# Who makes the low half of a weight slab while the expert gates are built: VectorE alone, or VectorE and GpSimd in turn

## The chip, the cores and the metric

The program runs on one core of a Trainium2 chip. The time is device microseconds (us) of one execution; a run's time is the median of several executions, and 2389.93 us is the median of three runs of the kernel before. TensorE does the matrix products, VectorE (DVE in the profile) the elementwise work, ScalarE (ACT) the copies, roundings and activations, GpSimd (POOL) a second stream of elementwise work, and SyncE (SP) issues the transfers of weights.

## The reference, cut to what matters

Two blocks of a network run one after the other on 256 tokens of width 1024. The change is in the last part of the first block, the expert layer, which picks 16 of 16384 single-neuron experts per token and head:

```python
u = expert_u[ec]                                     # the chosen experts' input rows
a = jax.nn.gelu(jnp.einsum('cd,chkd->chk', xc, u), approximate=False) * wc
return jnp.einsum('chk,chkd->cd', a, expert_v[ec])   # wc: softmax over the 16 chosen
```

## The kernel before, in words

The kernel doesn't gather the chosen experts. It computes all 16384 as 128 slabs of 128 experts and multiplies the activations by a dense gate that is zero where an expert wasn't chosen. Per slab there are 24 matmuls on the input side (`u_pair`, two slabs each, lines 600 to 606) and 24 on the output side (`v_pair`, lines 739 to 766).

**A weight slab** is 128 by 1024 numbers in float32. Every product is made from two parts that TensorE takes: a rounded high half and the rest, the low half. `slab` (lines 93 to 101) loads a slab (SyncE, tile `raw`, five buffers), rounds it on ScalarE (tile `whi`, two buffers, line 99) and subtracts on VectorE, or on the engine given as `lo_eng` (tile `wlo`, two buffers, line 100):

```python
nc.scalar.activation(hi[:, :n], raw[:, :n], AF.Copy)
(lo_eng or nc.vector).tensor_tensor(lo[:, :n], raw[:, :n], hi[:, :n], op=ALU.subtract)
```

Of a slab's 24 matmuls the first 16 read the high half and the last 8 the low half.

**The gate** is built twice, `gate(0)` and `gate(1)`, each for 64 of the 128 slabs. A gate goes through the tokens in 16 blocks of 16. For a block VectorE makes two tiles of ones and zeros in float16 (`e1` from `i1T`, `e2` from `i2T`, line 718) and multiplies the second by the gate values (`ep`, line 722), all from inputs in SBUF. TensorE multiplies them in 32 small matmuls (line 731), 16 into bank B and 16 into bank E, and after each 16 VectorE multiplies the result into the activations (two instructions of line 737, one input in PSUM, one in SBUF). Banks B and E have one buffer each; `e1`, `e2` and `ep` have two.

**The weave.** `weave` takes a step of the gate (four small matmuls) and a step of the weights in turn. `gate(0)` is woven with 16 input pairs (six matmuls a step), so that a block of tokens and a pair of slabs go together. `gate(1)` is woven with 16 output pairs (four matmuls a step); about eleven of them go with the gate and the other five stand behind its end. A `v_pair` also splits its activations (ScalarE line 129, VectorE line 130, tile `wl`). Between the two gates, and behind the second, pairs run without a gate. The build of the program fixes one order of instructions for each engine, which may differ from the order of the code; on the chip each engine takes its instructions strictly in that order, and waits where an input isn't ready or a buffer isn't free.

GpSimd makes low halves before the gates (lines 688 and 694 and the query weights) and nothing from then until the second block.

Of the kernel before, what the change touches and what calls it, by code (L numbers as in the profile page):

```python
# [37 lines left out]
def chained(*gens):  # L38
    for g in gens:
        yield from g  # L40


def weave(*gens):

    live = list(gens)
    while live:
        live = [g for g in live if next(g, live) is not live]


class Builder:  # L50
# [525 lines left out]
    def peer(self, x, ss):  # L576
        nc, tc, a = self.nc, self.tc, self.a
# [5 lines left out]
        with tc.tile_pool(name="peer", bufs=1) as pool:  # L583
# [11 lines left out]
            def expert(n):  # L595

                o = 2 * n % QT
                return A[2 * n // QT][:, o:o + 2]

            def u_pair(n, lo_eng=None):  # L600
                bk = self.bank("g")
                for e in range(2):
                    s = self.slab(a["peer_u"][2 * n + e], lo_eng=lo_eng)
                    for u_pair.mm in self.mm3_steps(bk[:, e * T:(e + 1) * T], s, hh, hl):
                        yield
                u_pair.act = nc.scalar.activation(expert(n), bk[:, :].rearrange("p (e t) -> p e t", e=2), AF.Gelu)

            def u_run(lo, hi, lo_eng=None):
                for _ in chained(*(u_pair(n, lo_eng) for n in range(lo, hi))):
                    pass  # L610

            quarter(0)
# [1 line left out]
            with tc.tile_pool(name="topk", bufs=1) as tp:  # L614
# [11 lines left out]
                for j in range(8):  # L626
                    q = tp.tile([128, 2, T], F32, tag="q", bufs=2, name=self.nm("q"))
# [79 lines left out]
            with tc.tile_pool(name="gate", bufs=1) as gpool:  # L707
# [28 lines left out]
                                g = bk[:, :].rearrange("p (t i) -> p i t", t=8)[:, QT * q:QT * q + QT]  # L736
                                nc.vector.scalar_tensor_tensor(w, g, 1.0 / 32768.0, w, op0=ALU.mult, op1=ALU.mult)

                def v_pair(n):
                    wh = gpool.tile([128, 2, T], F32R, tag="wh", bufs=2, name=self.nm("wh"))  # L740
                    wl = gpool.tile([128, 2, T], F32R, tag="wl", bufs=2, name=self.nm("wl"))
                    self.split(wh, wl, expert(n))
                    end = n == NI // 2 - 1

                    def terms(e):
                        hi, lo = self.slab(a["peer_v"][:, 2 * n + e])
                        return [(vs, ws, e) for vs, ws in ((hi, wh), (hi, wl), (lo, wh))]

                    def add(db, p, vs, ws, e):
                        nc.tensor.matmul(acc[db // 2][:, (db % 2) * T:(db % 2 + 1) * T],  # L750
                                         vs[:, db * 128:(db + 1) * 128], ws[:, e],
                                         start=n == 0 and p == 0 and db % 2 == 0,
                                         stop=end and p == 5 and db % 2 == 1)

                    if end:
                        last = terms(0) + terms(1)
                        for db in range(NC):
                            for p in range(6):
                                add(db, p, *last[p])
                    else:  # L760
                        for e in range(2):
                            for p, t in enumerate(terms(e)):
                                for db in range(NC):
                                    add(db, 3 * e + p, *t)
                                    if db % 4 == 3:
                                        yield

                quarter(2, gpool, 1)
                q = QT // 2
                weave(gate(0), chained(*(u_pair(n) for n in range(2 * q, 3 * q))))  # L770
                acc = [self.bank("s") for _ in range(4)]
                for _ in chained(*(v_pair(n) for n in range(q))):
                    pass
                quarter(3)
                u_run(3 * q, 4 * q)
                weave(gate(1), chained(*(v_pair(n) for n in range(q, 2 * q))))
                for _ in chained(*(v_pair(n) for n in range(2 * q, 4 * q))):
                    pass
                x2 = x
# [770 lines left out]
```

## Time and profile before

| | us |
|---|---|
| median of three runs (2389.66 to 2403.57) | 2389.93 |
| the profiled execution | 2403.91 |
| its span, first to last instruction | 2401.9 |
| TensorE busy in the span | 2286.2 (95%) |
| VectorE busy | 1558.1 (65%) |
| GpSimd busy | 319.1 (13%) |
| `gate(0)`, first to last small matmul | about 528 to 647 |
| `gate(1)` | about 831 to 924 |
| output pairs behind it | 924 to 1136 |

All stretches are us from the span's start, in the one profiled execution. An instruction's time in a timeline row is from its start to its end; consecutive VectorE instructions overlap by a tenth of a us or less, so the cost of one in a full queue is the distance to the start of the next. "Idle before" in a row is what the engine waited, with what ended the wait.

### The profile page before, as it was taken

The numbers are of one execution on the slowest core, as the hardware profiler recorded it, in microseconds if no ns is written. First come the engines' busy times: TensorE is split into PE (matmuls) and PEld (weight loads), VectorE is DVE, ScalarE is ACT, GpSimd is POOL, SyncE is SP. The second block draws the span as 40 slices with busy tenths as digits, with TensorE's granted clock in tenths as the row PEclk, the third lists the DMA queues.
The fourth block names the chain that finished last, engine by engine and source line by source line (L and its number), as shares of the span: only waits on it lengthen the run. The fifth ranks groups of instructions, "written<-read, shape, count | busy, mean of one in ns | idle before, by whom it ended". The sixth has DMA issues, their size and how long they took to land.

```text
span 2401.9 us, 48629 instructions
## 1 busy us (share of the span) xinstructions
PE 2286.2 (95%) x20688; PEld 2171.1 (90%) x20688; DVE 1558.1 (65%) x2387; ACT 1086.7 (45%) x1501; POOL 319.1 (13%) x226
## 2 busy tenths in 40 slices
PE   4999898999999989999999789999999999999999
PEld 3888898999999989999999678878999999888999
DVE  7667579448854497555765777325665765787664
ACT  4344444443344433445544554423544644555543
POOL 3001379500000000000000543211000000101000
PEclk7889899999999999999999788967999999999999
DMA  7766444554455535555556222202556556433555
GB/s 252 243 197 201 150 159 158 189 180 141 143 187 187 179 115 163 187 185 167 175 185 178 83 91 64 84 1 70 181 181 187 182 185 184 155 106 107 185 185 148
DMA packets 107756, 378.33 MB, mean 158 GB/s; under 512 B 12113, under 2 KB 15697, under 8 KB 107410
## 3 DMA queue, kind: packets, MB, share of 16 engines
q1 hardware_dynamic: 104224, 370.52, 48.2%
q10 hardware_dynamic: 3314, 4.70, 0.6%
q8 instruction: 162, 2.65, 0.5%
q14 instruction: 56, 0.46, 0.1%
HBM read 374.12 MB, written 1.05 MB: 156 GB/s over the span
## 4 chain that ended last, share of the span: by engine, by line
PE 77%; DVE 6%; POOL 2%; ACT 1%; issue 1%; POOLq 0%; DVEq 0%; ACTq 0%
PE bkA L126 25%; PE bkA L572 15%; PE bkB L126 11%; PE bkC L750 10%; PE bkD L750 4%; DVE wlo L100 1%; POOL wlo L100 1%; POOL b L865 1%; PE bkC L1349 1%; DVE e L718 1%; PE bkA L1185 1%; ACT whi L99 1%; PE bkB L731 0%; PE bkE L731 0%; DVE ep L722 0%
## 5 line engine op out<-in xcount | busy, mean ns | idle before, releaser
L99 ACT ACTIVATE whi<-raw 128x1024 fp32r<-128x1024 f32 (+1 forms) x664 | 695.6, 1048 | 999.7 <-PE bkA L126 284.8
L100 DVE TENSOR_TENSOR wlo<-raw,whi 128x1024 fp32r<-128x1024 f32 (+1 forms) x606 | 733.4, 1211 | 480.1 <-ACT whi L99 449.7
L126 PE MATMUL bkA<-xh,whi 128*128 128x256 f32 x1336 | 332.0, 287 | 14.8 <-ACT whi L112 7.0
L126 PE MATMUL bkA<-xl,whi 128*128 128x256 f32 x1336 | 331.4, 288 | 12.4 <-POOL xl L316 6.3
L126 PEld LDWEIGHTS bkA<-xh,whi 128*128 128x128 f32 x1336 | 255.7, 192 | 18.2 <-ACT whi L112 7.7
L126 PEld LDWEIGHTS bkA<-xl,whi 128*128 128x128 f32 x1336 | 255.5, 193 | 16.3 <-POOL xl L316 8.7
L572 PE MATMUL bkA<-xh,whi 128*128 128x256 f32 x1024 | 259.9, 290 | 0.0
L572 PE MATMUL bkA<-xl,whi 128*128 128x256 f32 x1024 | 251.6, 281 | 0.0
L572 PEld LDWEIGHTS bkA<-xl,whi 128*128 128x128 f32 x1024 | 193.3, 189 | 0.0
L572 PEld LDWEIGHTS bkA<-xh,whi 128*128 128x128 f32 x1024 | 193.2, 189 | 0.0
L126 PE MATMUL bkA<-xh,wlo 128*128 128x256 f32 x1336 | 187.4, 282 | 2.5 <-DVE wlo L100 2.5
L100 POOL TENSOR_TENSOR wlo<-raw,whi 128x1024 fp32r<-128x1024 f32 x58 | 155.6, 2694 | 197.0 <-DVE on L149 128.7
L126 PEld LDWEIGHTS bkA<-xh,wlo 128*128 128x128 f32 x1336 | 171.0, 190 | 3.1 <-DVE wlo L100 2.9
L126 PE MATMUL bkB<-xh,whi 128*128 128x256 f32 x624 | 157.3, 289 | 1.9 <-ACT whi L99 1.1
L572 PE MATMUL bkA<-xh,wlo 128*128 128x256 f32 x1024 | 149.7, 284 | 7.5 <-POOL wlo L100 7.5
L126 PE MATMUL bkB<-xl,whi 128*128 128x256 f32 x624 | 156.2, 288 | 0.0
L572 PEld LDWEIGHTS bkA<-xh,wlo 128*128 128x128 f32 x1024 | 132.2, 188 | 8.9 <-POOL wlo L100 8.9
L190 POOL TENSOR_TENSOR sq<-sq,sq 128x256 f32<-128x256 f32 (+1 forms) x15 | 17.5, 1164 | 902.0 <-ACT sq L188 685.0
L126 PEld LDWEIGHTS bkB<-xh,whi 128*128 128x128 f32 x624 | 120.8, 194 | 2.6 <-ACT whi L99 1.4
L126 PEld LDWEIGHTS bkB<-xl,whi 128*128 128x128 f32 x624 | 120.8, 194 | 0.2 <-issue 0.2
L126 PE MATMUL bkA<-hh,whi 128*128 128x256 f32 x484 | 117.8, 282 | 0.0
L126 PE MATMUL bkA<-hl,whi 128*128 128x256 f32 x484 | 117.5, 281 | 0.0
(649 smaller groups left out, 4533.8 us busy)
## 6 DMA issues: line engine op xcount, KB each, us to landing
raw<-in_ffn_in_dram SPq DMA_DIRECT2D x176, 512.0 KB, 3.5
raw<-in_peer_u_dram SPq DMA_DIRECT2D x128, 512.0 KB, 3.3
raw<-in_peer_v_dram SPq DMA_DIRECT2D x128, 512.0 KB, 3.7
raw<-in_ffn_out_dram SPq DMA_DIRECT2D x64, 512.0 KB, 3.6
rawm<-in_w_mod_dram SPq DMA_DIRECT2D x48, 512.0 KB, 4.3
raw<-in_w_in_dram SPq DMA_DIRECT2D x36, 512.0 KB, 4.5
raw<-in_ffn_out_dram SPq DMA_DIRECT2D x32, 384.0 KB, 3.1
raw<-in_w_query_dram SPq DMA_DIRECT2D x16, 512.0 KB, 3.3
```

The source lines that it names most:

```text
L99: nc.scalar.activation(hi[:, :n], raw[:, :n], AF.Copy)
L100: (lo_eng or nc.vector).tensor_tensor(lo[:, :n], raw[:, :n], hi[:, :n], op=ALU.subtract)
L126: nc.tensor.matmul(out, w[:, i], x[k0 + i], start=first and n == 0, stop=last and n == 3 * kn - 1)
L190: (nc.vector if c % 2 else nc.gpsimd).tensor_tensor(acc[c % 2], acc[c % 2], t, op=ALU.add)
L572: last = nc.tensor.matmul(out, w[:, i], x[i], start=j == 0, stop=j == 3 * NC - 1)
L718: nc.vector.tensor_tensor(e, idx[:, ts].rearrange("p (a b) -> p a b", b=2)[:, :, None].to_broadcast(shape), iota[:, None, i0:i0 + e.shape[ ...
L750: nc.tensor.matmul(acc[db // 2][:, (db % 2) * T:(db % 2 + 1) * T], vs[:, db * 128:(db + 1) * 128], ws[:, e], start=n == 0 and p == 0 and d ...
L865: nc.gpsimd.tensor_tensor(ll[:, c], t, hh[:, c], op=ALU.subtract)
L1185: nc.tensor.matmul(by[er, i], UV[ch][:, h], PM[A][1][:, ch, 2 * i + e], start=True, stop=S is None)
L1349: nc.tensor.matmul(o, qn[pr, h, 128 * i:128 * i + 128], kn[pr, h, :w], start=True, stop=False)
```

## The change

`u_pair` and `v_pair` get a list of engines for the low halves of their two slabs. In the two weaves the list is VectorE for the first slab and GpSimd for the second. Thirty-two subtractions move: 16 in `gate(0)`, 11 among the blocks of `gate(1)` (tiles wlo_9295 to wlo_10595) and five in the pairs behind it. Nothing else is added or removed; ScalarE's and SyncE's orders are the same as before.

```diff
-            def u_pair(n, lo_eng=None):
+            def u_pair(n, *lo_engs):
                 bk = self.bank("g")
                 for e in range(2):
-                    s = self.slab(a["peer_u"][2 * n + e], lo_eng=lo_eng)
+                    s = self.slab(a["peer_u"][2 * n + e], lo_eng=lo_engs[e % len(lo_engs)] if lo_engs else None)
...
-                def v_pair(n):
+                def v_pair(n, *lo_engs):
...
-                        hi, lo = self.slab(a["peer_v"][:, 2 * n + e])
+                        hi, lo = self.slab(a["peer_v"][:, 2 * n + e], lo_eng=lo_engs[e] if lo_engs else None)
...
-                weave(gate(0), chained(*(u_pair(n) for n in range(2 * q, 3 * q))))
+                weave(gate(0), chained(*(u_pair(n, nc.vector, nc.gpsimd) for n in range(2 * q, 3 * q))))
...
-                weave(gate(1), chained(*(v_pair(n) for n in range(q, 2 * q))))
+                weave(gate(1), chained(*(v_pair(n, nc.vector, nc.gpsimd) for n in range(q, 2 * q))))
```

VectorE's order in one block of `gate(0)` (an `e` from `i1T` is an `e1`, one from `i2T` an `e2`; A is the activations):

```order
 L737 SCALAR_TENSOR_TENSOR A_2639<-bkE_5666,A_2639 128x32x8
-L100 TENSOR_TENSOR wlo_5779<-raw_5777,whi_5778 128x1024
 L718 TENSOR_TENSOR e_770_5821<-i1T,iotaT 128x2048
 L722 TENSOR_TENSOR ep_5825<-e_771_5822,gp 128x2048
+L718 TENSOR_TENSOR e_795_6034<-i2T,iotaT 128x1024
 L737 SCALAR_TENSOR_TENSOR A_2638<-bkB_5721,A_2638 128x32x8
 L737 SCALAR_TENSOR_TENSOR A_2639<-bkB_5721,A_2639 128x32x8
 L100 TENSOR_TENSOR wlo_5836<-raw_5834,whi_5835 128x1024
-L718 TENSOR_TENSOR e_795_6034<-i2T,iotaT 128x1024
 L737 SCALAR_TENSOR_TENSOR A_2638<-bkE_5772,A_2638 128x32x8
 L737 SCALAR_TENSOR_TENSOR A_2639<-bkE_5772,A_2639 128x32x8
```

The subtraction behind the instructions of bank E left VectorE's queue, and the `e2` moved ahead of the instructions of bank B.

VectorE's order in the later blocks of `gate(1)`:

```order
-L100 TENSOR_TENSOR wlo_10208<-raw_10206,whi_10207 128x1024
+L718 TENSOR_TENSOR e_1295_10261<-i1T,iotaT 128x2048
 L722 TENSOR_TENSOR ep_10183<-e_1288_10180,gp 128x2048
-L718 TENSOR_TENSOR e_1295_10261<-i1T,iotaT 128x2048
+L718 TENSOR_TENSOR e_1296_10262<-i2T,iotaT 128x1024
+L130 TENSOR_TENSOR wl_10273<-A_2639,wh_10272 128x512
 L737 SCALAR_TENSOR_TENSOR A_5503<-bkB_10185,A_5503 128x32x8
 L737 SCALAR_TENSOR_TENSOR A_8228<-bkB_10185,A_8228 128x32x8
 L737 SCALAR_TENSOR_TENSOR A_5503<-bkE_10226,A_5503 128x32x8
 L737 SCALAR_TENSOR_TENSOR A_8228<-bkE_10226,A_8228 128x32x8
-L718 TENSOR_TENSOR e_1296_10262<-i2T,iotaT 128x1024
-L130 TENSOR_TENSOR wl_10273<-A_2639,wh_10272 128x512
```

One subtraction left, and the instructions with two inputs in SBUF now stand in a longer row ahead of those that read PSUM.

VectorE's order at the end of `gate(1)`:

```order
 L737 SCALAR_TENSOR_TENSOR A_8228<-bkB_10527,A_8228 128x32x8
-L100 TENSOR_TENSOR wlo_10595<-raw_10593,whi_10594 128x1024
+L130 TENSOR_TENSOR wl_10630<-A_2639,wh_10629 128x512
+L100 TENSOR_TENSOR wlo_10635<-raw_10633,whi_10634 128x1024
 L737 SCALAR_TENSOR_TENSOR A_5503<-bkE_10572,A_5503 128x32x8
 L737 SCALAR_TENSOR_TENSOR A_8228<-bkE_10572,A_8228 128x32x8
-L130 TENSOR_TENSOR wl_10630<-A_2639,wh_10629 128x512
-L100 TENSOR_TENSOR wlo_10635<-raw_10633,whi_10634 128x1024
-L100 TENSOR_TENSOR wlo_10665<-raw_10663,whi_10664 128x1024
 L130 TENSOR_TENSOR wl_10694<-A_2639,wh_10693 128x512
 L100 TENSOR_TENSOR wlo_10699<-raw_10697,whi_10698 128x1024
```

wlo_10595 is the last moved subtraction among the gate's blocks, wlo_10665 the first of the five behind them. On TensorE the small matmuls of `gate(1)` stood in 47 groups between weight matmuls, and stand in 68.

## Rows read from the trace of the kernel before

**Rows 1.** Busy us by stretch: before the gates, both gates, the pairs behind.
```profile
core 0: us, PE busy (x) PEld busy (x) DVE busy (x) ACT busy (x) POOL busy (x), PEclk, DMA share, GB/s
440.00:460.00 20.00, 20.00 (x172) 20.00 (x171) 1.67 (x2) 9.37 (x11) 14.09 (x6) 1.00 0.59 187
...
528.00:647.00 119.00, 119.00 (x1279) 113.21 (x1278) 103.10 (x140) 43.25 (x49) 0.00 (x0) 1.00 0.44 143
831.00:861.00 30.00, 30.00 (x343) 28.54 (x342) 27.24 (x39) 11.04 (x13) 0.00 (x0) 1.00 0.39 129
861.00:922.00 61.00, 51.21 (x642) 47.81 (x639) 60.58 (x92) 16.59 (x20) 0.00 (x0) 1.00 0.34 108
924.00:1136.00 212.00, 212.00 (x1791) 211.81 (x1791) 116.09 (x120) 98.54 (x115) 0.00 (x0) 1.00 0.57 188
```

**Rows 2.** Waits, 861 to 924: who waited for whom, us in total, times, longest.
```profile
PE bkD L750 <- DVE wl L130: 6.2, 4, 1.6
...
PE bkD L750 <- DVE wlo L100: 3.3, 3, 1.1
```

**Rows 3.** Timeline of VectorE, one block of gate(0): start, us, what, idle before.
```profile
543.17 1.23 DVE L100 TENSOR_TENSOR wlo<-raw,whi 128x1024 fp32r<-128x1024 f32 x1
544.31 1.22 DVE L718 TENSOR_TENSOR e<-i1T,iotaT 128x2048 f16<-128x2048 f16 x1
545.45 1.22 DVE L722 TENSOR_TENSOR ep<-e,gp 128x2048 f16<-128x2048 f16 x1
546.58 0.75 DVE L737 SCALAR_TENSOR_TENSOR A<-bkB,A 128x256 f32<-128x256 f32 x2
547.25 1.21 DVE L100 TENSOR_TENSOR wlo<-raw,whi 128x1024 fp32r<-128x1024 f32 x1
548.38 0.68 DVE L718 TENSOR_TENSOR e<-i2T,iotaT 128x1024 f16<-128x1024 f16 x1
549.78 0.76 DVE L737 SCALAR_TENSOR_TENSOR A<-bkE,A 128x256 f32<-128x256 f32 x2 [0.72 <-PE bkE L731]
550.63 1.23 DVE L100 TENSOR_TENSOR wlo<-raw,whi 128x1024 fp32r<-128x1024 f32 x1
```

**Rows 4.** Timeline of VectorE in gate(1), a recurring instruction, first and fourth.
```profile
861.16 0.75 DVE L737 SCALAR_TENSOR_TENSOR A<-bkB,A 128x256 f32<-128x256 f32 x2
...
916.72 0.74 DVE L737 SCALAR_TENSOR_TENSOR A<-bkB,A 128x256 f32<-128x256 f32 x2
```

**Rows 5.** Groups of GpSimd's line 100, 284 to 341, then 384 to 425.
```profile
L100 POOL TENSOR_TENSOR wlo<-raw,whi 128x1024 fp32r<-128x1024 f32 x17 | 40.6, 2391 | 19.7 <-ACT whi L99 17.3 <-PE bkA L126 2.5
...
L100 POOL TENSOR_TENSOR wlo<-raw,whi 128x1024 fp32r<-128x1024 f32 x12 | 44.3, 3723 | 0.3 <-ACT whi L99 0.3
```

**Rows 6.** Timeline of VectorE in the second of those stretches.
```profile
401.86 4.38 DVE L682 TENSOR_TENSOR eq<-bf,i 128x2048 f32<-128x2048 f32 x1
406.28 4.35 DVE L684 TENSOR_TENSOR eq<-eq,IF 128x2048 f32<-128x2048 f32 x1
410.67 2.29 DVE L686 TENSOR_REDUCE sel<-eq 128x128 f32<-128x2048 f32 x1
412.99 4.38 DVE L682 TENSOR_TENSOR eq<-bf,i 128x2048 f32<-128x2048 f32 x1
```

**Rows 7.** Timelines of GpSimd and of VectorE, 342 to 351.
```profile
342.33 2.41 POOL L100 TENSOR_TENSOR wlo<-raw,whi 128x1024 fp32r<-128x1024 f32 x1 [0.44 <-ACT whi L99]
...
342.45 2.57 DVE L649 TENSOR_TENSOR cand<-V 128x256 f32<-128x256 f32 x1
...
350.60 0.28 DVE L651 TENSOR_TENSOR cand<-V 128x128 f32<-128x128 f32 x1
```

**Rows 8.** Timelines of VectorE and of GpSimd in the second block of the network.
```profile
1462.98 0.68 DVE L1011 TENSOR_TENSOR t2b<-bkC,t2b 128x512 f32<-128x512 f32 x1
...
1463.20 1.29 POOL L955 TENSOR_TENSOR t2g<-t2g,b 128x512 f32<-128x512 f32 x1 [2.14 <-DVE b L954]
```

**Rows 9.** Busy us by stretch (columns as in rows 1), the second block of the network.
```profile
1430.00:1440.00 10.00, 6.76 (x243) 6.16 (x244) 9.93 (x11) 3.86 (x5) 4.85 (x6) 0.92 0.37 121
1440.00:1450.00 10.00, 9.03 (x232) 8.55 (x221) 8.81 (x17) 2.51 (x4) 2.55 (x2) 0.74 0.18 56
```

More of the change, by code (lines that the diff above doesn't have):

```diff
@@ L606, in u_pair, with u_run @@
                 u_pair.act = nc.scalar.activation(expert(n), bk[:, :].rearrange("p (e t) -> p e t", e=2), AF.Gelu)
-            def u_run(lo, hi, lo_eng=None):
-                for _ in chained(*(u_pair(n, lo_eng) for n in range(lo, hi))):
+            def u_run(lo, hi, *lo_engs):
+                for _ in chained(*(u_pair(n, *lo_engs) for n in range(lo, hi))):
                     pass
```

## The prediction

> **What bounds the kernel now.** I read the share of each engine by stretch first, because the change touches only two stretches and the averages of the whole span say nothing about them. In `gate(0)`, 528 to 647, TensorE is busy for all of its 119 us and VectorE for 103 [rows 1]: TensorE sets the pace, and the 16 subtractions that leave VectorE there can't shorten anything. In `gate(1)` it turns. From 861 to 922 VectorE is busy for 60.58 of 61 us and TensorE for 51.21 [rows 1], and the table of waits says whom TensorE waits for: `wl` and `wlo`, both VectorE's, 9.5 us together [rows 2]. So 61 - 51.2 = 9.8 us of TensorE's time are lost to VectorE, and that is all that the change can win: 0.4% of the kernel. Behind the gate, 924 to 1136, TensorE is full again [rows 1].
>
> Next I looked for what the new owner costs. Alone, GpSimd takes 2.39 us for a low half (the first group of [rows 5]), against steps of 1.13 to 1.14 us in VectorE's full queue [rows 3]. While GpSimd made every low half before the gates, with VectorE nearly idle, TensorE was still full (20.00 of 20 us, 440 to 460 [rows 1]), since a slab's low half is read last and there are two buffers. Its length by itself does no harm.
>
> What matters is what the two engines do to each other, and the trace has met that case. Between 384 and 425, with VectorE at line 682 and 684, GpSimd's same subtraction took 3.72 us on average instead of 2.39 [rows 5], and VectorE's 2048-element instructions with two SBUF inputs took 4.38 and 4.35 us, while the one with a single input, over as many elements, took 2.29 [rows 6]. The clearest row is earlier: at 342.45 a 256-element instruction of line 649 took 2.57 us, and it ended 0.28 us after GpSimd's subtraction of 342.33 (342.33 + 2.41 = 344.74) [rows 7]; 0.28 us is what its neighbour of half the size takes when nothing is in the way [rows 7]. It stood still until GpSimd was done. So two-input instructions and GpSimd's subtraction **take turns**, whole instruction by whole instruction. An instruction with one input in PSUM is not held: line 1011 took 0.68 us for 512 elements beside GpSimd's line 955 at 1.29 us [rows 8].
>
> **The change part by part.** In the gates the two-input SBUF instructions are lines 100, 130, 718 and 722; line 737 reads PSUM. The instructions of 718 and 722 are float16, and no row shows a float16 one beside GpSimd. The bounds are that they are not held, or held like the float32 ones of rows 6 and 7. I take held: every row of a two-input SBUF instruction that met GpSimd's subtraction is stretched, and nearest in form is line 682, a comparison with a repeated operand, as line 718 is.
>
> The Trainium skill's page "SBUF — State Buffer", section "Who interferes with whom", says that a VectorE instruction with two SBUF inputs contends with a GpSimd instruction that reads SBUF, whichever is first holding the shared ports to its end, and makes no exception for a type. By that rule float16 is held and the sum below stands; by the float32 rows alone it would be that of the second rival.
>
> *`gate(0)`, 16 moved.* A block takes 550.63 - 543.17 = 7.46 us and VectorE waits for 0.72 of it [rows 3], so its own work is 6.74. Without one subtraction it is 5.60; with GpSimd's 2.40 in turn, 8.00; with one pair of line 737 (0.67, from 546.58 to 547.25 [rows 3]) beside GpSimd, 7.33. That is below 7.46, so I put 0. If nothing runs beside GpSimd it is (8.00 - 7.46) x 16 = +8.6, the upper end.
>
> *`gate(1)`, 11 moved among its blocks.* VectorE's queue is full: from 861.16 to 916.72 are three repeats of 18.52 us [rows 4], each with three blocks and two pairs. Each moved subtraction takes away 1.14 and brings 2.40 of standing still: +1.26, and 11 x 1.26 = +13.9. If the standstill is rather the 2.1 us that line 682 lost (4.38 - 2.29 [rows 6]), it is 11 x 0.96 = +10.6. Against that stands cover: VectorE still had 30 - 27.24 = 2.8 us free between 831 and 861 [rows 1], and where GpSimd's turn falls on line 737, 0.67 us each run beside it. GpSimd starts when ScalarE's half is ready, which is bound to neither kind of instruction; I give the pairs of line 737 five of the eleven: 3.4 us. So 13.9 - 2.8 - 3.4 = **+7.7**, and 4.4 with the shorter standstill. Ends: 10.6 - 2.8 - 11 x 0.67 = +0.4, and 13.9 - 2.8 = +11.1. TensorE can't absorb it: the small matmuls and `wl` come from VectorE, so the gate's end moves with VectorE's queue, and the same pairs stand behind it. The wait that goes (VectorE's second subtraction) is replaced by `ep`, `wl` and the first slab's `wlo` coming later.
>
> *The five behind `gate(1)`.* When GpSimd kept up with TensorE alone, a slab went by in 0.44 + 2.41 = 2.85 us [rows 7]; now it makes one in two. In turn with VectorE's one subtraction and `wl` (0.7, half a line 100) a pair asks 2.4 + 1.14 + 0.7 = 4.2 of 5.7 us. Cost 0, and what hides it is TensorE's own work. ScalarE's and SyncE's orders don't change; a `raw` buffer comes free about 2 us later than before, with five of them and transfers at 0.34 to 0.44 of their engines' time in the gates [rows 1], so 0.
>
> The sum is +7.5, between the two standstills and nearer the larger. The profiled execution took 2403.91 us, so it would be 2411.4; that execution is 14.0 above the median of 2389.93, which becomes **2397.4**. About 1%, 24 us, is what can be told from no change here, so the forecast is a small loss that counts as no change.
>
> **The rivals.**
>
> *Relief.* No turns at all for this mix: VectorE's three blocks shrink by 2 x 1.14 from 18.52 to 16.24, and TensorE's share of them is 18.52 x 51.2 / 61 = 15.5, so 2.28 of every 3.0 lost come back: 9.8 x 2.28 / 3.0 = 7.5, 2382.4. For it speaks only that no float16 row was met; `wlo` and `wl` are float32, and rows 6 and 7 speak against it. The Trainium skill's "Perfetto Trace Analysis", section "Optimizing Scalar/DVE Operations", says that moving work to GpSimd may make sense when VectorE is saturated, and adds that the shared read port may make it useless; the first half alone is this rival. Chance 0.08.
>
> *Only float32 is held.* Then GpSimd runs beside 718 and 722 for free, over half of VectorE's work in a block, and is stopped by, or stops, 100 and 130 alone. Each turn costs VectorE between 0 and 2.40 us, in the middle 1.2, which is what the move saves: 0, so 2390. Chance 0.17.
>
> *The turns reach line 737, and `gate(0)` tips.* If an instruction of line 737 is held as well (it has one SBUF input, and rows 8 are one meeting only), or its pairs never fall beside GpSimd, both gates pay in full: 8.6 + 11.1 = +19.7, 2409.6. It decides where VectorE's block in `gate(0)` passes 7.46 us. It becomes over 1% if a turn is longer than 2.40: all 27 moved subtractions pay, so (23.9 - 19.7) / 27 = 0.16 more, a standstill above 2.56 us. Part of it could come from TensorE's clock: it was granted 1.00 at 84% busy [rows 1], but 0.92 and then 0.74 around a stretch of 68% busy [rows 9]. With +7.7 on 92 us TensorE stays near 80%, so I leave the clock at 1.00. Chance 0.15.
>
> That the change doesn't do what it says is excluded by the order of instructions, which has the 32 on GpSimd.
>
> **How the numbers follow.** Forecast 0.60 (2390 to 2401 by its ends), only float32 0.17, relief 0.08, full price 0.15. The likeliest gives 2397.4. The range goes from 2383, which leaves out most of relief (2382.4), to 2410, which leaves out the upper part of the full price. Faster by over 1% needs 24 us where at most 9.8 can be won: 0.01. Slower by over 1% is two fifths of the last rival: 0.06. Within 1%: 0.93.
>
> **What would show it.** In the new profile GpSimd's subtractions in the gates should last 2.4 to 3.6 us, not 2.39; some instructions of 718, 722, 130 and 100 should last 2.1 to 2.4 us longer than their 1.22 and 0.68, the float16 ones among them; line 737 should keep its 0.75 a pair. `gate(0)` should keep its 119 us with TensorE full. `gate(1)` should grow from 93 to about 100 us, three blocks from 18.5 to 20 or 21 us in its full part, with more idle TensorE before lines 731 and 750, and the pairs behind keep 212 us. Float16 instructions of unchanged length would make the forecast wrong downwards; a `gate(0)` over 121 us, upwards.

## The result and the profile after

| | before | after |
|---|---|---|
| median, same chip, 15 executions each | 2388.59 | 2403.94 |
| lowest to highest | 2377.21 to 2403.57 | 2392.01 to 2415.92 |
| ratio | | 1.0066 [1.0043, 1.0088] |
| first small matmul of `gate(0)` to the last matmul of line 750 | 608.1 | 620.8 |

The change costs 0.66%, some 16 us with an interval of 10 to 21: a small loss, inside the 1% that counts as no change and inside the range, at about twice the +7.5 that the sum gave. The ratio is an estimate from all executions of both kernels, not the quotient of the two medians.

The rest of the kernel, ahead of the changed part and behind it, differed by 9 and by 22 us between two executions of one and the same kernel (the kernel after, and e2 below). So the stage that holds the change is compared by itself: from the first start of line 731 to the last start of line 750, read from the groups of those two lines (start of the first, start of the last). It took 608.1 us before, 620.8 after and 620.6 in a second profile of the same kernel: **+12.5 to +12.7 us**. All "stages" below are this distance.

Where in the stage? The busy time by stretch (columns as in [rows 1]): of the kernel after `gate(0)`, `gate(1)`, and the pairs behind. The stretch called `gate(1)` here and below runs from the first matmul of the output pairs that are woven with the gate to the last small matmul; 27 of the gate's 512 small matmuls ran ahead of it already, just behind `gate(0)`, and 485 are in it.

```profile
core 0: us, PE busy (x) PEld busy (x) DVE busy (x) ACT busy (x) POOL busy (x), PEclk, DMA share, GB/s
528.00:647.00 119.00, 118.60 (x1280) 112.72 (x1279) 115.44 (x126) 43.94 (x50) 38.90 (x16) 1.00 0.42 139
828.90:933.80 104.90, 90.37 (x996) 84.59 (x996) 97.39 (x122) 28.90 (x33) 29.38 (x11) 0.92 0.35 111
933.80:1147.30 213.50, 213.50 (x1797) 213.13 (x1796) 118.16 (x115) 98.76 (x115) 11.99 (x5) 1.00 0.57 183
```

and `gate(1)` of the kernel before, cut at the same two instructions:

```profile
830.50:923.40 92.90, 83.11 (x996) 78.21 (x995) 89.37 (x131) 28.87 (x33) 0.00 (x0) 1.00 0.36 115
```

`gate(0)` kept its length with TensorE full: from its first small matmul, at 526.2 here and at 528.0 before, its 1281 matmuls fill 119.3 us in both. (The row is cut at the times of the kernel before.) VectorE is busy for 115 instead of 103 us of it. The pairs behind take 213.5 against 213.0 us. `gate(1)` holds the loss: 92.9 became 104.9. VectorE's own work there grew by 8.0 us (89.37 to 97.39), although eleven subtractions had left it, and its idle time grew from 3.5 to 7.5. TensorE needed 7.3 us more for the same 996 matmuls, at a granted clock of 0.92 instead of 1.00. GpSimd's eleven subtractions take 2.67 us each.

What stretched VectorE is read from its groups by shape, 829 to 935 in the kernel after (busy us, mean ns of one | idle before them):

```profile
L718 DVE TENSOR_TENSOR e<-i1T,iotaT 128x2048 f16<-128x2048 f16 x14 | 20.5, 1463 | 0.0
L100 DVE TENSOR_TENSOR wlo<-raw,whi 128x1024 fp32r<-128x1024 f32 x11 | 20.0, 1819 | 3.2 <-ACT whi L99 1.9 <-issue 1.3
L722 DVE TENSOR_TENSOR ep<-e,gp 128x2048 f16<-128x2048 f16 x14 | 18.6, 1326 | 0.0
L718 DVE TENSOR_TENSOR e<-i2T,iotaT 128x1024 f16<-128x1024 f16 x12 | 13.9, 1168 | 0.0
L737 DVE SCALAR_TENSOR_TENSOR A<-bkE,A 128x256 f32<-128x256 f32 x32 | 11.9, 412 | 3.4 <-PE bkE L731 3.3
...
L130 DVE TENSOR_TENSOR wl<-A,wh 128x512 fp32r<-128x512 f32 x10 | 8.3, 834 | 0.0
```

In the kernel before, the same groups have means of 1215, 1217, 1217, 681, 416 and 682 ns. So 14 x 0.248 + 11 x 0.602 + 14 x 0.109 + 12 x 0.487 + 10 x 0.152 = 19.0 us of standing still: 1.73 for each of GpSimd's eleven. Line 100 has ten fewer in this stretch (21 before) and line 130 one more (0.6), so 19.0 - 10 x 1.14 + 0.6 = +8.2, about the 8.0 read above. The four kinds with two inputs in SBUF are all stretched, the float16 ones too; line 737, with one input in PSUM, isn't.

One by one it looks like this, VectorE first and then GpSimd (start, us, what, idle before):

```profile
882.23 0.74 DVE L737 SCALAR_TENSOR_TENSOR A<-bkB,A 128x256 f32<-128x256 f32 x2
882.89 0.74 DVE L737 SCALAR_TENSOR_TENSOR A<-bkE,A 128x256 f32<-128x256 f32 x2
883.56 2.79 DVE L722 TENSOR_TENSOR ep<-e,gp 128x2048 f16<-128x2048 f16 x1
...
891.24 1.22 DVE L722 TENSOR_TENSOR ep<-e,gp 128x2048 f16<-128x2048 f16 x1
892.37 3.42 DVE L100 TENSOR_TENSOR wlo<-raw,whi 128x1024 fp32r<-128x1024 f32 x1
...
901.05 2.85 DVE L718 TENSOR_TENSOR e<-i2T,iotaT 128x1024 f16<-128x1024 f16 x1
...
904.42 0.74 DVE L737 SCALAR_TENSOR_TENSOR A<-bkB,A 128x256 f32<-128x256 f32 x2
```
```profile
882.88 2.38 POOL L100 TENSOR_TENSOR wlo<-raw,whi 128x1024 fp32r<-128x1024 f32 x1 [6.40 <-PE bkC L750]
892.05 2.65 POOL L100 TENSOR_TENSOR wlo<-raw,whi 128x1024 fp32r<-128x1024 f32 x1 [6.79 <-ACT whi L99]
900.18 3.17 POOL L100 TENSOR_TENSOR wlo<-raw,whi 128x1024 fp32r<-128x1024 f32 x1 [5.47 <-ACT whi L99]
```

At 882.88 GpSimd begins beside a pair of line 737, which keeps its length; the float16 instruction behind the pair ends at 886.35, 1.09 us after GpSimd's end at 885.26, where alone it takes 1.21. At 892.05 GpSimd itself stands first, while `ep` ends, and takes 2.65 instead of 2.38 us; then line 100 stands, and ends at 895.79, again 1.09 after GpSimd's 894.70. Turns, whole instruction by whole instruction. The repeat of three blocks, 18.52 us in [rows 4], is 904.42 - 882.23 = 22.2 here, and the next one as well. The first of the two holds three turns; the second holds two, and a wait of 1.54 us for bank E at 911.52, shown further down.

Who waits for whom, 831 to 940 in the kernel after (us, times, longest):

```profile
PE bkB L731 <- DVE ep L722: 7.3, 7, 1.8
...
PE bkD L750 <- DVE wl L130: 4.1, 2, 2.0
PE bkD L750 <- DVE wlo L100: 2.8, 3, 1.0
...
DVE A L737 <- PE bkE L731: 3.3, 2, 1.8
```

`wlo` and `wl`, 9.5 us in [rows 2], are down to 6.9, and none of it is GpSimd's `wlo`. But `ep`, which had cost TensorE nothing, now takes 7.3 us, and VectorE in turn waits 3.3 us for bank E, where it had waited 0.5.

### The profile page after: what moved, and what is told of

The parts are those of the page before. It is cut to its first block, busy times and chain, and to the rows that moved or that the text cites. A ratio compares the mean times of both kernels' runs of the same rounds, so it can differ in the third digit from the quotient of the medians.

```text
span 2404.0 us, 48631 instructions
## 1 busy us (share of the span) xinstructions
PE 2284.2 (95%) x20688; PEld 2172.5 (90%) x20688; DVE 1579.0 (66%) x2355; ACT 1086.1 (45%) x1501; POOL 399.9 (17%) x258
## 3 DMA queue, kind: packets, MB, share of 16 engines
q8 instruction: 162, 2.65, 0.4%
## 4 chain that ended last, share of the span: by engine, by line
PE 76%; DVE 7%; POOL 2%; ACT 2%; issue 1%; DVEq 0%; POOLq 0%; ACTq 0%
PE bkA L126 25%; PE bkA L572 15%; PE bkB L126 11%; PE bkC L750 10%; PE bkD L750 4%; DVE wlo L100 1%; DVE e L718 1%; POOL wlo L100 1%; POOL b L865 1%; PE bkC L1349 1%; ACT whi L99 1%; DVE ep L722 1%; DVE A L737 1%; PE bkE L731 1%; PE bkA L1185 1%
## 5 line engine op out<-in xcount | busy, mean ns | idle before, releaser
L100 DVE TENSOR_TENSOR wlo<-raw,whi 128x1024 fp32r<-128x1024 f32 (+1 forms) x574 | 703.2, 1226 | 464.1 <-ACT whi L99 433.6
L100 POOL TENSOR_TENSOR wlo<-raw,whi 128x1024 fp32r<-128x1024 f32 x90 | 237.3, 2644 | 623.9 <-ACT whi L99 397.2
L750 PE MATMUL bkC<-wh,whi 128*128 128x256 f32 x768 | 117.8, 284 | 0.0
```

## The experiments

The **theory**: VectorE's instructions with two SBUF inputs and GpSimd's subtraction take turns; that lengthens VectorE's queue in `gate(1)`, where it is full, and costs nothing where TensorE is full. The **rivals**: `gate(0)` pays a part; the loss comes from the order of instructions that the change brought, not from the turns; the five subtractions behind the gate cost something; TensorE's lower clock carries much of it.

| run | us | ratio to before | stage | against 608.1 | `gate(1)` |
|---|---|---|---|---|---|
| after | 2403.94 | 1.0066 [1.0043, 1.0088] | 620.8 | +12.7 | 104.9 |
| after, once more (one execution) | 2396.22 | | 620.6 | +12.5 | 105.0 |
| e1: only `gate(0)` | 2385.35 | 1.0011 [0.9980, 1.0041] | 608.4 | +0.3 | 93.0 |
| e2: only the second weave | 2396.47 | 1.0040 [1.0013, 1.0068] | 617.9 | +9.8 | 102.4 |
| e2, once more (one execution) | 2418.34 | | 620.1 | +12.0 | 104.4 |
| e3: twice on VectorE | 2401.02 | 1.0062 [1.0032, 1.0091] | 618.1 | +10.0 | 102.5 |
| e4: GpSimd only writes | 2383.10 | 0.9988 [0.9964, 1.0013] | 600.3 | -7.8 | 85.1 |
| e5: gate spread over more pairs | 2382.66 | 0.9984 [0.9962, 1.0005] | 599.5 | -8.6 | 108.8 |
| e6: the same with GpSimd | 2389.46 | 1.0009 [0.9987, 1.0031] | 609.1 | +1.0 | 118.1 |
| e8: GpSimd behind the gate | 2388.57 | 1.0004 [0.9982, 1.0026] | 609.6 | +1.5 | 92.9 |
| e9: e2 with extra matmuls | 2403.31 | 1.0050 [1.0020, 1.0080] | 622.0 | +13.9 | 106.8 |
| e7: e2 in two halves (one execution) | 2384.94 | | 614.9 | +6.8 | 99.6 |
| e10: small matmuls in sixteens | 2362.10 | 0.9884 [0.9844, 0.9925] | 583.6 | -24.5 | 103.6 |

The interval of a ratio is 10 to 19 us wide, so most of these verdicts rest on the stage, of which each run has one profile. Between two profiles of the same kernel it differed by 0.2 us (after) and 2.2 us (e2). The last column compares like with like only from the first row to e4, and for e7 and e8: e5, e6 and e10 weave more pairs into the gate, e9 and e10 have small matmuls in it that ran ahead of it before, and e9 has extra ones.

**Which gate pays?** Each weave alone gets GpSimd. In the first run the second weave is as before,

```diff
-                weave(gate(0), chained(*(u_pair(n) for n in range(2 * q, 3 * q))))
+                weave(gate(0), chained(*(u_pair(n, nc.vector, nc.gpsimd) for n in range(2 * q, 3 * q))))
```

> Only the 16 subtractions in gate(0) go to GpSimd; gate(1) is as before. Theory (turns on two-input SBUF instructions, cover in gate(0)): VectorE's block there is 7.33 us against TensorE's 7.46, so gate(0) keeps 119 us and the time stays within 2 us of before. Rival (both gates pay, nothing runs beside GpSimd): 8.00 us a block, +8.6 us.

in the second run the first weave:

```diff
-                weave(gate(1), chained(*(v_pair(n) for n in range(q, 2 * q))))
+                weave(gate(1), chained(*(v_pair(n, nc.vector, nc.gpsimd) for n in range(q, 2 * q))))
```

> Only the 16 of the second weave go to GpSimd; gate(0) is as before. Theory: this carries all of the loss, so the ratio is that of the whole change, 1.0066, about +12 to +16 us, with the first small matmul of gate(1) to the last in about 104 us instead of 93, and TensorE's granted clock below 1.00 somewhere in that stretch. Rival (the change costs in both gates): 3 to 8 us less than the whole change.

The first stage is 608.4, the second 617.9, and 620.1 in a second profile. The second run's +9.8 is just under the +12 that the theory expected, and its 2.9 us less than the whole change is just short of the rival's 3; the second profile, with +12.0, leaves 0.7. VectorE stands still in `gate(0)` as much as in `gate(1)`; its stretch and its most stretched group in the first run:

```profile
520.70:640.00 119.30, 119.30 (x1281) 113.51 (x1280) 113.89 (x123) 43.34 (x49) 40.17 (x16) 1.00 0.41 142
```
```profile
L718 DVE TENSOR_TENSOR e<-i1T,iotaT 128x2048 f16<-128x2048 f16 x15 | 44.5, 2965 | 0.0
```

Nearly every one of these float16 instructions takes 2.97 us on the mean instead of 1.22, and the gate lasts the 119.3 us that it lasted before (528.0 to 647.3), because TensorE never waits. The loss is `gate(1)`'s: 12.0 of 12.7 us by the rows of the kernel after, and +0.3 for the first weave against +9.8 or +12.0 for the second by these runs.

**Turns, or only a longer queue?** Here GpSimd gets nothing, and VectorE makes the moved subtraction twice, so that its queue grows by an instruction where the change makes it stand still.

```diff
-        (lo_eng or nc.vector).tensor_tensor(lo[:, :n], raw[:, :n], hi[:, :n], op=ALU.subtract)
+        for _ in range(1 + (lo_eng == "twice")): (nc.vector if lo_eng in (None, "twice") else lo_eng).tensor_tensor(lo[:, :n], raw[:, :n], hi[:, :n], op=ALU.subtract)
...
+                weave(gate(1), chained(*(v_pair(n, nc.vector, "twice") for n in range(q, 2 * q))))
```

> GpSimd does nothing; in the second weave VectorE makes the low half of every second slab twice, with the same result. If a turn of GpSimd's costs VectorE's queue its 2.4 us and nothing else counts, this is the same price: 11 x 1.14 = 12.5 less the 2.8 us that were free = +9.7 us, and a few more if the clock falls as in the changed kernel; gate(1) takes 103 to 106 us. If the loss lies in GpSimd itself (its low half is late, its signals are slow), VectorE's second copy doesn't have that, and the loss is under half, +6 or less.

The stretch of `gate(1)`:

```profile
829.60:932.10 102.50, 86.98 (x996) 79.94 (x995) 100.56 (x141) 29.41 (x33) 0.00 (x0) 0.98 0.31 105
```

The stage's +10.0 is what was expected, with a `gate(1)` of 102.5 us just below the 103 to 106. It is about as slow as the move to GpSimd, without any GpSimd, so more of VectorE's time in this queue is enough to give a loss of this size. There is a difference worth keeping: VectorE worked 11.2 us more than before and sat idle for only 1.9 us instead of 3.5, so cover was used up, as the prediction had it. With GpSimd it worked 8.0 us more and sat idle longer.

**The move without the turns.** GpSimd fills the tile with zeros three times instead of subtracting (the low-half product of every second slab of this weave is left out). VectorE's order stays that of the move. Not all waits do, though the expectation says so: the fill reads neither `raw` nor `whi`, so it doesn't wait for ScalarE, and begins as soon as its buffer is free.

```diff
+        [nc.gpsimd.memset(lo[:, :n].bitcast(F32), 0.0) for _ in range(3)] if lo_eng == "fill" else (lo_eng or nc.vector).tensor_tensor(lo[:, :n], raw[:, :n], hi[:, :n], op=ALU.subtract)
...
+                weave(gate(1), chained(*(v_pair(n, nc.vector, "fill") for n in range(q, 2 * q))))
```

> In the second weave GpSimd writes zeros three times into the low half of every second slab and reads nothing: the low half's product is left out there, with all waits kept. Theory (only a GpSimd instruction that reads SBUF holds VectorE's two-input instructions): VectorE is relieved, lines 718, 722, 130 and 100 keep their 1.22 and 0.68 us, and the time falls by about 7 us, gate(1) to 85 us. Rival (any GpSimd instruction holds them): they are stretched by 1 to 2.4 us and the time rises by 5 us or more.

Its `gate(1)`, one of GpSimd's fills, and VectorE at that time and as groups:

```profile
826.80:911.90 85.10, 82.27 (x996) 78.41 (x995) 78.34 (x122) 28.88 (x33) 31.52 (x33) 1.00 0.40 132
```
```profile
881.73 2.97 POOL L100 MEMSET wlo<- 128x1024 f32 x3 [4.37 <-PE bkC L750]
```
```profile
881.07 1.22 DVE L722 TENSOR_TENSOR ep<-e,gp 128x2048 f16<-128x2048 f16 x1
882.20 1.22 DVE L100 TENSOR_TENSOR wlo<-raw,whi 128x1024 fp32r<-128x1024 f32 x1
```
```profile
L718 DVE TENSOR_TENSOR e<-i1T,iotaT 128x2048 f16<-128x2048 f16 x14 | 17.1, 1219 | 0.0
L100 DVE TENSOR_TENSOR wlo<-raw,whi 128x1024 fp32r<-128x1024 f32 x11 | 13.4, 1222 | 2.5 <-ACT whi L99 2.4
```

GpSimd is busy for longer than with the subtractions (31.5 against 29.4 us), a subtraction of VectorE's falls inside its fill and keeps its 1.22 us, and no group is stretched. The stage is 7.8 us **shorter** than before, where the prediction's relief rival said 7.5. So the new order costs nothing, and 17.6 to 19.8 us of the second weave's time (7.8 and the 9.8 or 12.0 of e2) come from GpSimd's reading subtraction: from the turns, which are what is seen to go, and what follows from them. That a late `wlo` from GpSimd costs nothing is not shown here, since the fill isn't late; it is read from the waits of the kernel after, where TensorE never waits for GpSimd. The Trainium skill's page "SBUF — State Buffer", section "Who interferes with whom", says that a two-input VectorE instruction contends with a GpSimd instruction that reads SBUF and not with one that only writes it. The trace agrees on both sides: 3.42 us beside the subtraction, 1.22 beside the fill.

**Does it matter that VectorE is full?** In this pair of runs the gate's steps are spread over more pairs of slabs, first without GpSimd, then with it.

```diff
+                def paced(g):
+                    for i, _ in enumerate(g):
+                        yield
+                        if i % 5 in (1, 3):
+                            yield
...
+                weave(paced(gate(1)), chained(*(v_pair(n) for n in range(q, 2 * q))))
```

> VectorE keeps every low half, as before; gate(1) is spread over 15 of its 16 pairs instead of 11 (two empty steps in every seven of its weave). Theory: gate(1) is lost time because VectorE has 18.5 us of work for three blocks and two pairs; with a block for each pair it has about 4.2 + 2.9 = 7.1 us against TensorE's 7.5 (48 weight matmuls at 0.118 and 32 small ones in eights of four), so TensorE sets the pace and the 9.8 us come back but for some 2 to 3 us of more changes between the kinds of matmul: -7 us from the first small matmul of gate(0) to the last of the output pairs. Rival (the loss isn't VectorE's share but the chain from block to block): no change.

```diff
+                weave(paced(gate(1)), chained(*(v_pair(n, nc.vector, nc.gpsimd) for n in range(q, 2 * q))))
```

> As the run before, with GpSimd on every second slab of the second weave. Theory: a block and a pair cost VectorE 7.1 - 1.14 + 2.4 less up to 0.67 beside line 737, 7.7 to 8.4 us, over TensorE's 7.5 again: 15 x 0.2 to 0.9 = 3 to 13 us slower than the paced kernel without GpSimd. Rival (GpSimd is a relief wherever VectorE is not full): the same or faster than that kernel.

Their `gate(1)`, without and with GpSimd:

```profile
823.90:932.70 108.80, 107.08 (x1200) 103.13 (x1198) 102.58 (x145) 40.25 (x45) 0.00 (x0) 1.00 0.43 141
```
```profile
824.80:942.90 118.10, 113.37 (x1200) 107.04 (x1200) 111.53 (x130) 40.48 (x46) 41.62 (x15) 0.99 0.40 135
```

Spreading makes TensorE nearly full (107.1 of 108.8 us, 713 matmuls of the output pairs beside the 485 small ones instead of 509) and wins 8.6 us of stage: most of the 9.8 us that the prediction read as the most to be won were there, and needed no second engine. With GpSimd 9.6 us go again. VectorE's work grew by 9.0 us (which makes 1.74 for each of fifteen turns, less 15 x 1.14), and of the 6.2 us that it had free in the gate nothing was used: it has 6.6 free with GpSimd. Free time on VectorE isn't cover here, and with a granted clock of 0.99 it isn't TensorE's clock that takes it.

**The pairs behind the gate.** GpSimd gets every second slab there, in all 32 pairs, and nothing in the weaves.

```diff
-                for _ in chained(*(v_pair(n) for n in range(2 * q, 4 * q))):
+                for _ in chained(*(v_pair(n, nc.vector, nc.gpsimd) for n in range(2 * q, 4 * q))):
```

> No GpSimd in either weave; it makes the low half of every second slab of the 32 output pairs behind gate(1), where VectorE has 3.0 us of work in 5.7. Theory: 2.4 + 1.14 + 0.7 = 4.2 of 5.7 us, hidden under TensorE: no change, under 1 us between the first small matmul of gate(0) and the last of the output pairs. Rival (GpSimd's low halves come too late for TensorE): up to 0.5 us for each of the 32, +16 us.

The stage grew by 1.5 us where less than 1 was expected. The table of waits has one entry of TensorE for GpSimd:

```profile
PE bkD L750 <- POOL wlo L100: 1.3, 1, 1.3
```

It is the very last pair, whose high and low products are interleaved, so that the low half is wanted at once. That leaves 0.2 for the other 31 pairs. Five such pairs, as in the change, cost nothing that can be seen; the length of GpSimd's instruction shows only where no other matmul stands between.

**The clock.** In `gate(1)` of the kernel after, TensorE waits, and its clock falls. Two pieces of it:

```profile
853.10:865.10 12.00, 10.22 (x103) 9.43 (x100) 10.20 (x16) 3.10 (x4) 2.92 (x2) 0.86 0.25 85
901.10:913.10 12.00, 9.50 (x100) 8.97 (x101) 10.46 (x16) 1.08 (x2) 2.25 (x1) 0.72 0.28 89
```

In the kernel before it is 1.00 through the whole gate [rows 1]. Waits alone don't tell it: in e3 TensorE waited for 15.5 of the gate's 102.5 us, in the kernel after for 14.5 of 104.9, and the granted clock is 0.98 there and 0.92 here. To see what it costs, I first gave TensorE extra matmuls to do in its waits (eight a block, into a bank that the block's own overwrite), with the second weave on GpSimd:

```diff
-                            bk = self.bank("t")
+                            bk = self.bank("t"); [nc.tensor.matmul(bk[:, :T], hh[f][:, :128], hl[f], start=True, stop=True) for f in range(NC if r and not h else 0)]
```

> GpSimd in the second weave alone (as in the run with gate(1) only), and eight extra matmuls ahead of the small ones of each block of gate(1), into a bank that is overwritten behind them: 15 x 8 x 0.118 = 14.2 us more for TensorE where it has most of its waits. Theory (part of the loss is TensorE's clock at 1.2 GHz after its waits, 10 us of it in that run, which cost up to 5): the granted clock stays nearer 1.00 in gate(1) and the stage is no longer than without the extra matmuls, 0 to -4 us, although 14 us of work were added. Rival (the clock costs nothing, VectorE alone sets the time): granted clock as before, and the stage the same or longer by up to 5 us.

```profile
831.20:938.00 106.80, 103.09 (x1140) 96.65 (x1139) 98.68 (x123) 29.39 (x33) 31.09 (x11) 1.00 0.33 109
```

The clock stayed at 1.00, and yet the stage was 4.1 us longer than without the extra work, against an expected 0 to -4. That falls to the rival's number, but not to its reason (it had the clock as before): the extra matmuls also wait for bank B (3.7 us) and make VectorE wait for it (3.6 us). It settles nothing about the clock.

Then the two kernels once more, for two executions with different clocks:

> The changed kernel once more, for a second profile of the same program. From the first small matmul of gate(0) to the last of the output pairs the kernel before took 608.1 us, the changed one 620.8 with TensorE at 1.2 GHz for about 17 us of gate(1), and gate(1) alone in the weave 617.9 with about 10 us. Theory (the fall of the clock is part of the loss, up to half of the time at 1.2 GHz): the stage differs from 620.8 by 0.3 to 0.5 us for each us more or less at 1.2 GHz. Rival (it doesn't matter): within 1 us of 620.8, whatever the clock.

> The kernel with GpSimd in the second weave alone, once more, for the same purpose: 617.9 us with about 10 us at 1.2 GHz in the first profile; by the theory 0.3 to 0.5 us more or less for each us more or less at 1.2 GHz, by the rival within 1 us of 617.9.

The kernel after had 620.6 against 620.8, at a clock of 0.94 and 0.92 in the gate: the rival's answer. The other one did differ, 620.1 against 617.9 at a clock of 0.92 and 0.95, by about what the theory asks for, and there the place can be seen. Its `gate(1)` in the first and the second execution, with VectorE's wait for bank E in each:

```profile
823.30:925.70 102.40, 87.50 (x996) 81.91 (x994) 97.01 (x122) 28.90 (x33) 29.37 (x11) 0.95 0.34 114
```
```profile
DVE A L737 <- PE bkE L731: 1.2, 2, 0.9
```
```profile
831.10:935.50 104.40, 90.12 (x996) 84.41 (x995) 96.95 (x122) 28.92 (x33) 29.36 (x11) 0.92 0.35 111
```
```profile
DVE A L737 <- PE bkE L731: 3.3, 2, 1.8
```

VectorE's work is equal to 0.1 us; the gate is 2.0 us longer, TensorE's matmuls took 2.6 longer, and VectorE waited 2.1 more for bank E. Its waits stand at the same five instructions in both executions, and only the two for bank E differ. In the kernel after, VectorE's second wait of this kind and TensorE's rows show what stands in it, and two rows of e2 (the first of the two executions) the same matmuls at a granted clock of 1.00:

```profile
911.52 0.76 DVE L737 SCALAR_TENSOR_TENSOR A<-bkE,A 128x256 f32<-128x256 f32 x2 [1.54 <-PE bkE L731]
```
```profile
908.56 0.78 PE L750 MATMUL bkD<-wh,wlo 128*128 128x256 f32 x2
909.13 1.48 PE L750 MATMUL bkC<-wh,wlo 128*128 128x256 f32 x6
910.41 0.63 PE L750 MATMUL bkD<-wh,whi 128*128 128x256 f32 x2
910.84 0.54 PE L750 MATMUL bkC<-wh,whi 128*128 128x256 f32 x2
911.22 0.26 PE L731 MATMUL bkE<-ep,e 128*128 128x64 f16 x3
```
```profile
823.58 0.88 PE L750 MATMUL bkC<-wh,whi 128*128 128x256 f32 x6
824.29 0.39 PE L750 MATMUL bkD<-wl,whi 128*128 128x256 f32 x2
```

Bank E's last three small matmuls stand behind twelve weight matmuls, which took 911.22 - 908.56 = 2.66 us at the lower clock level, 1.2 GHz; where the clock is granted in full, at 2.4 GHz, twelve take 1.42 (six are followed by the next 824.29 - 823.58 = 0.71 us after their start). VectorE stood 1.54 us for them, so the lower clock makes up 1.24 of this wait. A slow TensorE thus makes the full VectorE wait. Between these two executions that is 2 us; the 2.8 us by which the wait for bank E grew from before to after (0.5 to 3.3) is the most that I can give to it. The second profile of the kernel after has 0.9 us less of this wait (2.4) at the same stage, but VectorE worked 0.6 us more there (98.03 against 97.39) and waited 0.4 for bank B; the two can cancel, and the split isn't sharp.

**A shorter instruction.** The subtraction on GpSimd in two of half the length, second weave only:

```diff
+        for o in ((0, 512) if lo_eng == "halves" else (0,)): (nc.gpsimd if lo_eng == "halves" else lo_eng or nc.vector).tensor_tensor(lo[:, o:n if lo_eng != "halves" else o + 512], raw[:, o:n if lo_eng != "halves" else o + 512], hi[:, o:n if lo_eng != "halves" else o + 512], op=ALU.subtract)
```

> As the run with GpSimd in the second weave alone, with each of GpSimd's subtractions in two instructions of 512 elements. Theory (turns by whole instructions): VectorE stands still for two turns of about 1.3 us instead of one of 2.4, and in between it gets one instruction through; the sum is the same, so the stage is 617.9 +- 3 us, and the stretched instructions of VectorE are about 1.2 us longer than alone instead of 2.2. Rival (it is the length of a single turn that hurts): the stage falls to 612 or less.

```profile
821.80:921.40 99.60, 87.72 (x996) 82.43 (x994) 92.87 (x122) 28.89 (x33) 39.56 (x22) 0.95 0.36 116
```
```profile
L718 DVE TENSOR_TENSOR e<-i1T,iotaT x32: 1205/1216/2302, 453.9 to 909.4; 128x2048 f16<-128x2048 f16 x32
```

The longest float16 instruction (least, median and most ns in the second row) has 1.1 us more than alone, not 2.2: what is held is held for one instruction of the other engine. VectorE's work is 4.1 us less than with whole ones, GpSimd's busy time 10.2 more, and the stage 3.0 less than in the first profile of e2, at the edge of what was expected as no difference, and 5.2 less than in the second. It is one execution, so I take the halved standstill from it, not the gain.

**A faster version.** If TensorE and VectorE both are nearly full in the gates, what is left to take away is work. In the kernel before, the first weight matmul behind a group of small ones takes 0.20 us to the next instead of 0.12 (559.85 to 560.05), so the gates give way after 16 small matmuls instead of 4, without GpSimd:

```diff
-                                if t % 2:
+                                if t == 7:
                                     yield
...
+                def paced(g, k):
+                    for i, _ in enumerate(g):
+                        for _ in range(k + (k == 5 and i % 2)):
+                            yield
...
+                weave(paced(gate(0), 4), chained(*(u_pair(n) for n in range(2 * q, 3 * q))))
...
+                weave(paced(gate(1), 5), chained(*(v_pair(n) for n in range(q, 2 * q))))
```

> No GpSimd; both gates spread over their pairs as in the paced run, and sixteen small matmuls (one bank) in a row instead of four. In the trace of before four small matmuls cost 0.22 us with the change to and from the weight matmuls and thirty-two in a row about 1.3, so sixteen should cost about 0.67 where four fours cost 0.89: 0.2 x 32 = 7 us less for each gate, as long as VectorE keeps up (6.7 us of a gate(0) block's 7.0). With the paced run's -8.6 us in gate(1): -13 to -20 us, a ratio of 0.992 to 0.995. Rival (VectorE sets the pace as soon as TensorE is faster, and banks B and E with one buffer each hold the bursts): no better than the paced kernel, 0.998.

Its `gate(0)`:

```profile
520.20:627.50 107.30, 107.30 (x1265) 106.04 (x1264) 101.20 (x139) 40.97 (x48) 0.00 (x0) 1.00 0.47 154
```

2362.1 us, a ratio of 0.9884 [0.9844, 0.9925]: faster than both kernels. `gate(0)` went from 119.3 to 107.3 us, but with 16 weight matmuls fewer in it (1265 for 1281 matmuls), which come behind its last small one: at 0.118 each they are 1.9 us, so the same matmuls took about 10 us less. TensorE's rows, of the kernel before and of this one, account for nearly all of it:

```profile
560.65 0.29 PE L731 MATMUL bkB<-ep,e 128*128 128x64 f16 x4
560.78 0.96 PE L572 MATMUL bkA<-xh,wlo 128*128 128x256 f32 x6
561.58 0.29 PE L731 MATMUL bkE<-ep,e 128*128 128x64 f16 x4
```
```profile
561.22 0.66 PE L731 MATMUL bkB<-ep,e 128*128 128x64 f16 x16
564.65 0.66 PE L731 MATMUL bkE<-ep,e 128*128 128x64 f16 x16
```

Four small matmuls and the six weight matmuls behind them take 561.58 - 560.65 = 0.93 us; four times that, for sixteen and 24, is 3.72. Sixteen in a row and 24 weight matmuls behind them take 564.65 - 561.22 = 3.43. That is 0.29 us in each of 32 groups of sixteen, 9.3 us. The stage gained 24.5 us, beyond the 13 to 20 that I expected: 10 here, and the 8.6 of e5 for spreading `gate(1)`, leave about 6 for the sixteens in `gate(1)`, which were not measured by themselves.

## Why the prediction was right, and where it was short

*The number*: 2403.94 is inside the range, but above the 2390 to 2401 that the forecast itself had by its ends, and a little nearer to the full-price rival's 2409.6 than to the forecast's 2397.4. `gate(1)` grew by 12.0 us, beyond the upper end of +11.1, and its three blocks took 22.2 us instead of 20 or 21. So the total by itself doesn't tell the forecast from that rival; the stage of e1 and the rows of line 737 do. Two errors of opposite sign, below, kept the sum as near as it is, which is luck.

*Where the loss falls*: right. `gate(0)` 0 (e1: +0.3), the pairs behind 0 (213.5 against 213.0, and e8 with one late low half at the very end), all of it in `gate(1)`.

*The turns*: right. The choice between bounds, that float16 instructions are held as the float32 ones, is confirmed (2.79 us for line 722, 2.85 for `e2`; e4 for the reason). Line 737 isn't held (a mean of 412 ns, 416 before), so the last rival's mechanism isn't there. The rival "only float32" fell with the float16 rows. (Its "over half of VectorE's work in a block" for lines 718 and 722 is 2.9 of 6.7 us by [rows 3], under half; no price hangs on it.) Relief fell too, but its price was near: 7.5, and e4 shows 7.8 where the turns are taken away.

*The price of a turn*: a little too high. The sum had 2.40, and 0.67 back in five of eleven: 2.1 on average. Measured are 1.73. The long standstills are 2.17 to 2.21 us (2.85 - 0.68 and 3.42 - 1.21), nearer to the lower bound, the 2.1 lost by line 682 [rows 6], and GpSimd itself stands in some of the turns. VectorE's work grew by 8.0 us, where 13.9 - 3.4 = 10.5 were forecast.

*The cover*: this term failed. I took 2.8 us off because VectorE had that much free from 831 to 861 [rows 1], and counted on no new wait. In place of that, VectorE's idle time **grew** by 4.0 us: 6.8 us on the wrong side, more than the 2.5 by which the work was too high. Together they make 7.7 + 6.8 - 2.5 = 12.0, what `gate(1)` shows. e3 shows that a steady addition does use up cover (1.6 us of it). In the kernel after a part of it was used as well: the waits for banks B and E that VectorE had there before, 1.4 us up to 851, are gone. But new ones came: 3.3 us for bank E instead of 0.5, 2.8 instead of 1.6 at the gate's start for ScalarE, and 1.3 near its end for which the profile names no cause.

*The clock*: left at 1.00, wrong. It was 0.92 in the gate. I named it in the last rival and gave it no price, since TensorE had 1.00 in a stretch where it was 84% busy. In the kernel after it was 86% busy in `gate(1)`, and the two pieces shown above have 0.86 and 0.72; in e3 it was 85% busy at 0.98. The busy share of the gate was no guide. What the clock costs is part of the idle term above: 2 us between two executions of e2, none to be seen between two of the kernel after, up to 2.8 by the wait for bank E. How much of the loss it carries stays open within these bounds.

The Trainium skill's "Perfetto Trace Analysis", section "Optimizing Scalar/DVE Operations", warns that work moved from VectorE to GpSimd might not help because of the shared port. The trace agrees and goes further: it hurt, since each 1.14 us taken away came back as 1.73.

## What to carry to other kernels

Before moving an elementwise instruction with SBUF inputs from a full VectorE to GpSimd, count the VectorE instructions beside it that read two SBUF tensors, float16 ones as well as float32: each moved instruction then costs VectorE most of GpSimd's duration (1.73 of 2.4 us here), and pays only if that is less than what it took itself. Don't subtract VectorE's free time as cover for turns: it wasn't cover in the kernel after or in e6, though e3's steady addition used some of it. Why turns bring new waits is argued, not shown: TensorE and VectorE wait for each other through banks B and E, and no run gave these a second buffer. Look also whether the new gaps come with a lower TensorE clock. When two engines are both nearly full, spreading their work evenly (8.6 us), or that together with fewer changes between kinds of matmul (24.5 us), gave more than GpSimd did even without turns (7.8 us).

## What the runs showed of the hardware

- float16 instructions with two SBUF inputs stand still beside GpSimd's subtraction as float32 ones do (`ep` at 883.56: 2.79 us instead of 1.21; a mean of 2.97 for line 718 in e1); beside a GpSimd instruction that only writes they don't (1.22).
- The hold lasts one GpSimd instruction: with halves (one execution) the longest one of line 718 took 2.30 us, where whole ones held instructions of the same length (1.22) for up to 3.42.
- Four float16 matmuls and six float32 ones behind them took 0.93 us, sixteen and 24 took 3.43 instead of four times that, 3.72.
- TensorE's granted clock, 1.00 through the whole `gate(1)` before, fell to 0.72 in a piece of the kernel after where TensorE was busy for 9.5 of 12 us, and was at 1.00 again in the pairs behind.
